# The three score blocks of a head pair: one burst or several on TensorE, in a hybrid decoder layer

## The chip, the cores and the metric

The kernel runs on one core of a Trainium2 chip. The metric is the device time of one execution in microseconds (us); the time of a kernel is the median of its runs. A profiled execution gives a page and a trace, in which every instruction stands with its start, its duration, its line in the kernel's file and what it waited for. The engines are TensorE (matmuls, with its weight loads as a row of their own), VectorE, ScalarE, GpSimd and SyncE, which issues most DMAs. In the profile they are PE, PEld, DVE, ACT, POOL and SP.

## The reference

One layer of a decoder over 1024 positions of 1024 channels, in float32:

```python
h = rms_norm(x, norm_mix)
xa, ga, q, f, v, g, m_a, m_b = split(h @ w_in)
y_a = rg_lru(conv4(xa)) * gelu(ga)                   # recurrence by channel
qf  = silu(q);  f_gate = lb + (1 - lb) * sigmoid(f)  # 8 heads of 128 channels
kf  = (1 - lb) * sigmoid(-f)
o   = hgrn2(qf, kf, log(f_gate), v)                  # gated linear attention
y_b = rms_norm(o) * silu(g)
x   = x + (sigmoid(m_a) * y_a + sigmoid(m_b) * y_b) @ w_out
h   = rms_norm(x, norm_mlp)
x   = x + square(relu(h @ w_up)) @ w_down
return rms_norm(x, norm_final)
```

The part that matters here is `hgrn2`. Per head it is causal attention without a softmax, in which the weight of position s for a later position t is the product of the gates between them:

```python
scores[t, s] = sum_k qf[t, k] * kf[s, k] * prod(f_gate[s+1 .. t, k])   # s <= t
o[t]         = sum_s scores[t, s] * v[s]
```

## The kernel before, in words

**The products.** Matrices are multiplied in float32 out of two parts each, a high one and the rest; `mm3` (line 142) issues the three matmuls of a product, lines 144 to 146. A product over the whole width of 512 columns is 0.4 us long in the trace's rows and starts a little over 0.2 us after the one before.

**The head pairs.** The mixer works on 512 positions (c = 0 or 1) of two heads (p = 0 to 3) at a time. I call these eight pieces of work head pairs and number them 4c + p, 0 to 7. For each there is a `stage(i)` (line 818), a Python generator which projects `v` of the pair before, then `xa`, `q` and `f` of its own pair and the gates of the recurrence, and which yields after every few matmuls; and `hgrn(c, p, ...)` (line 556), which makes the attention of a pair out of the projected `q`, `f` and `v`. The loop at line 942 runs `hgrn` of pair i while stage i + 1 (for pair 7, `last_stage`) is used to fill its gaps: `go(n)` inside `hgrn` lets the stage go on by n yields. A yield is called a step here. In a stage from the second on, the first 16 steps belong to `v` (six matmuls of 256 columns each), the next eight to `xa`, the next eight to `q` (six matmuls of 512 columns each), and so on. TensorE executes exactly in the order in which the Python code issues: `pin` (line 138) ties each of its instructions to the one before.

**The scores.** Inside chunks of 128 positions the scores are put together from blocks at several distances, because the product of gates between two positions is factored into a part on the side of `q` and a part on the side of `k`. Three sets of small matmuls, made by `blocks` (line 563), come first: `pt1` out of `q1` and `kk`, `pt2` out of `qa` and `kb`, `pt8` out of `qb` and `kc`. Each set is 32 matmuls with a stationary block of 32 columns and 48 moving columns; a float32 matmul is two records in the trace, so that a set is a burst of 64 on line 570. VectorE makes the operands: the products on line 560, the last of them for `pt8` in `level_q` (line 623). Afterwards VectorE takes the results out: `own_block(pt1)` (lines 576 to 581), `level_blocks(0, ...)` for `pt2` and `level_blocks(1, ...)` for `pt8` (line 589), between them products that turn `kc` and `qb` into the operands of the next distances (32 and 64, matmuls at lines 690 and 701). These follow after `go(at[1])`; transposes of `k` (line 727), the products `k` by `v` (737) and the output (762, 765) follow at `go(at[2])`, `go(at[3])` and `go(at[4])`.

**PSUM.** Its eight banks go under three tags: `pj` with four (projections), `sc` with two (`pt1`, `pt2`, the blocks of distance 64, one of the four `v` sums, one half of the recurrence's gates), `hg` with two (`pt8`, the blocks of distance 32, all transposes, `k` by `v`, the output). A bank comes free when its last reader is done.

**What else is in a stage.** The second half of the positions is normalised and transposed while the first half is worked on. `transposed` (line 174) takes one tile of 128 rows: four transposes into one bank of `hg`, four into another (line 178); `split` (line 86) then copies each bank's content on ScalarE (line 87) and subtracts the copy from it on VectorE (line 88). In stage 2 this is done for one tile behind the fourth step of `xa`, that is behind step 20, and in stage 3 for two, behind its steps 18 and 22 (`hooks`, line 830). In stage 1 one is done between `xa` and `q`.

**VectorE and ScalarE.** Their order is found by the framework's planner at build time, which takes instructions as they become ready in its own estimate, those traced earlier first, those under `high_priority` (lines 106 and 827) ahead of that.

The steps at which the bursts stand come from tables:

```python
GO = (26, 5, 3, 1, 1)                # pairs 1, 2, 3
GO_FIRST = (16, 5, 2, 1, 2)          # pair 0
GO_SECOND_HALF = (26, 7, 3, 1, 1)    # pairs 4 to 7
```

The first entry is the step of the third burst; the first stands four steps before it, the second two.

## Time and profile before

| | |
|---|---|
| median of 3 runs | 1543.05 us (1542.97 to 1544.44) |
| profiled execution | 1542.76 us |
| its span, first to last instruction | 1541.0 us |
| granted TensorE clock, mean | 0.999 |
| TensorE busy | 1524.6 us, 99% |
| VectorE busy | 1150.3 us, 75% |
| ScalarE busy | 810.2 us, 53% |
| GpSimd busy | 153.8 us, 10% |

A row of the timeline gives start, duration, engine, line, operation, output and inputs, their sizes, and in brackets the idle time before it and what ended that. A row of the groups gives engine, line, operation and shapes with a count, then busy us, the mean ns of one, and the idle time before. Names are those of the program's tiles without their numbers: `sc` is a bank for scores, `xT_x` one for the transposes of `x`. TensorE's rows are pipelined: an instruction starts before the one ahead of it ends, so that the distance of starts is what it costs.

### The profile page before, as it was taken

What the parts mean: (1) busy time and instruction counts of PE and PEld (TensorE: products, weight loads), DVE (VectorE), ACT (ScalarE), POOL (GpSimd) and SP (SyncE); (2) the same over time, 40 slices, a digit from 0 to 9 for tenths busy, and PEclk for the clock granted to TensorE, in tenths of its full rate; (3) what the DMA queues carried; (4) which work ended last, traced back from release to release, by engine and by line L of the source; (5) the groups of instructions that cost most, each with busy time, mean ns of one, the idle gap of its engine ahead of it and who ended that gap; (6) DMA issues with size and microseconds to landing.
All of it is one profiled execution on the core that took longest, in us unless ns stands there. A gap on an engine that the chain in (4) does not pass through costs nothing. (4 is left out here: it accounts for less than half of the span.)

```text
span 1541.0 us, 23190 instructions
## 1 busy us (share of the span) xinstructions
PE 1524.6 (99%) x9081; PEld 1273.8 (83%) x9081; DVE 1150.3 (75%) x1656; ACT 810.2 (53%) x1341; POOL 153.8 (10%) x188
## 2 busy tenths in 40 slices
PE   8999999999999999999999999999999999999997
PEld 7878988889889887888888888888888778888886
DVE  5798595485675838786856578888888898888877
ACT  6656757568567335454533447667767721111115
POOL 1022210232614600000000000000000000000000
PEclk9999999999999999999999999999999999999999
DMA  8545455465664274432338324666666675666642
GB/s 300 188 160 192 151 192 192 150 220 169 228 229 142 99 298 164 150 137 82 137 103 330 127 109 161 264 247 248 249 248 248 231 296 224 244 257 252 250 184 109
DMA packets 81679, 306.82 MB, mean 199 GB/s; under 512 B 8481, under 2 KB 20897, under 8 KB 68642
## 3 DMA queue, kind: packets, MB, share of 16 engines
q1 hardware_dynamic: 77536, 292.75, 51.6%
q10 hardware_dynamic: 4034, 12.59, 2.1%
q8 instruction: 71, 1.16, 0.3%
q14 instruction: 38, 0.31, 0.1%
HBM read 201.50 MB, written 103.81 MB: 198 GB/s over the span
## 5 line engine op out<-in xcount | busy, mean ns | idle before, releaser
L1559 DVE TENSOR_TENSOR acc<-acc,dX 128x512 f32<-128x512 f32 x128 | 85.3, 685 | 29.9 <-PE dX L146 27.4
L87 ACT CAST wA<-q 128x512 fp32r<-128x512 f32 x46 | 28.6, 622 | 147.9 <-PE dX L146 101.6
L88 DVE TENSOR_TENSOR wL<-raw,wH 128x1024 fp32r<-128x1024 f32 x48 | 58.7, 1224 | 43.2 <-ACT wH L87 43.0
L87 ACT CAST wH<-raw 128x1024 fp32r<-128x1024 f32 x48 | 50.4, 1051 | 36.4 <-DMA raw<-wts_in 14.7
L1559 DVE TENSOR_TENSOR acc<-acc,dY 128x512 f32<-128x512 f32 x64 | 43.5, 686 | 13.1 <-PE dY L146 12.9
L144 PE MATMUL po<-wH,y 128*128 128x512 f32 x128 | 49.8, 393 | 0.0
L145 PE MATMUL po<-wL,y 128*128 128x512 f32 x128 | 49.8, 389 | 0.0
L146 PE MATMUL po<-wH,y 128*128 128x512 f32 x128 | 49.7, 390 | 0.0
L1420 ACT ACTIVATE b<-b 128x512 f32<-128x512 f32 x48 | 30.2, 630 | 32.2 <-DVE b L1419 32.1
L88 DVE TENSOR_TENSOR wA<-q,wA 128x512 fp32r<-128x512 f32 x46 | 31.5, 687 | 15.4 <-ACT wA L87 15.3
L108 ACT CAST wH<-raw 128x1024 fp32r<-128x1024 f32 x36 | 37.7, 1049 | 8.2 <-issue 3.7
L171 POOL TENSOR_TENSOR rstd_h<-rstd_h,mhalf 128x1 f32<-128x1 f32 x8 | 4.6, 585 | 371.9 <-DVE rstd_h L166 371.9
L465 DVE SCALAR_TENSOR_TENSOR xc<-xp,pvt,xc 128x512 f32<-128x512 f32 x48 | 40.0, 844 | 1.1 <-ACT xc L449 1.1
L981 DVE TENSOR_TENSOR s<-q,q 128x512 f32<-128x512 f32 x46 | 31.6, 687 | 4.9 <-DMA q<-mlp_in 4.6
L378 POOL TENSOR_TENSOR stt<-r,stt 128x256 fp32r<-128x256 f32 x16 | 19.9, 1262 | 126.3 <-ACT stt L377 114.2
L989 DVE TENSOR_TENSOR s<-q 128x512 f32<-128x512 f32 x46 | 31.6, 687 | 0.4
L1421 ACT ACTIVATE b<-b 128x512 f32<-128x512 f32 x48 | 30.2, 631 | 1.2
L769 ACT ACTIVATE on<-po 128x128 f32<-128x128 f32 x64 | 16.9, 278 | 26.1 <-PE po L765 26.0
L146 PEld LDWEIGHTS po<-wH,y 128*128 128x128 f32 x128 | 24.0, 188 | 5.0
L145 PEld LDWEIGHTS po<-wL,y 128*128 128x128 f32 x128 | 24.1, 188 | 4.8
L144 PEld LDWEIGHTS po<-wH,y 128*128 128x128 f32 x128 | 24.0, 188 | 4.8
L1071 DVE TENSOR_TENSOR gb<-gY,ge 128x512 f32<-128x512 f32 x14 | 9.7, 690 | 23.3 <-PE gY L146 23.3
(2546 smaller groups left out, 5448.6 us busy)
## 6 DMA issues: line engine op xcount, KB each, us to landing
q<-mlp_in SPq DMA_DIRECT2D x92, 512.0 KB, 3.7
raw<-wts_in SPq DMA_DIRECT2D x80, 512.0 KB, 4.7
rest<-wL SPq DMA_DIRECT2D x36, 512.0 KB, 2.8
wL<-rest SPq DMA_DIRECT2D x36, 512.0 KB, 4.0
hd<-ri SPq DMA_DIRECT2D x16, 256.0 KB, 3.5
od<-onT ACTq DMA_DIRECT2D x8, 512.0 KB, 6.9
cdT<-stT SPq DMA_DIRECT2D x16, 256.0 KB, 3.1
o<-od SPq DMA_DIRECT2D x4, 1024.0 KB, 7.3
```

Of the source, the lines that this page charges most:

```text
L87: keep(A.copy(h, src))
L88: ins = V.tensor_tensor(out=lo, in0=src, in1=h.bitcast(F32), op=ALU.subtract)
L108: A.copy(h, raw)
L144: pin(PE.matmul(o, ah, bh, start=first, stop=False, **how))
L145: pin(PE.matmul(o, ah, bl, start=False, stop=False, **how))
L146: pin(PE.matmul(o, al, bh, start=False, stop=last, **how))
L465: ins = V.scalar_tensor_tensor(xc[:, s, :], xp[:, j : j + T], pvt[:, PV_CW + 8 * j + u : PV_CW + 8 * j + u + 1], xc[:, s, :], op0=ALU.mult ...
L981: ins = V.tensor_tensor(out=sa[:, 0, :], in0=a21, in1=a22, op=ALU.add)
L989: V.tensor_tensor(out=sb[:, 0, :], in0=a21, in1=a11, op=ALU.add)
L1420: A.activation(b[:, at, :], b[:, at, :], AF.Relu, scale=-1.0 if at == 2 else 1.0)
L1421: A.activation(b[:, at, :], b[:, at, :], AF.Square)
L1559: V.tensor_tensor(out=dst, in0=dst, in1=banks[bk, pr], op=op)
```

## The change

A table says for six of the eight pairs how many steps to go before the first burst, between the first and the second, and between the second and the third; pairs 3 and 6 take the default. The first number counts from the place where the first burst stood. What is put before the bursts or between them is taken off the steps that follow the third, so that everything behind `go(at[1])` keeps its step.

```diff
+SCORES_AT = {0: (1, 0, 3), 1: (-4, 0, 0), 2: (3, 0, 0), 4: (2, 0, 0), 5: (0, 0, 0), 7: (3, 0, 0)}
...
         at = GO_FIRST if first else GO_SECOND_HALF if c else GO
-        between = 2
-        go(at[0] - 2 * between)
+        before_1, before_2, before_8 = SCORES_AT.get(4 * c + p, (0, 0, 4))
+        go(at[0] - 4 + before_1)
         pt1 = blocks(kk, lambda k: q1[:, 16 * k : 16 * k + 16, :], "1")
-        go(between)
+        go(before_2)
         pt2 = blocks(kb, lambda k: qa[:, k * g0 // 32 : (k + 1) * g0 // 32, 1:7, :], str(c0))
-        go(between)
+        go(before_8)
         pt8 = blocks(kc, lambda k: q4[:, k * g1 // 32 : (k + 1) * g1 // 32, 1:7, :], str(c1), "hg")
...
-        go(at[1])
+        go(at[1] + 4 - before_1 - before_2 - before_8)
```

| pair | bursts at steps, before | after |
|---|---|---|
| 0 | 12, 14, 16 | 13, 13, 16 |
| 1 | 22, 24, 26 | 18, 18, 18 |
| 2 | 22, 24, 26 | 25, 25, 25 |
| 3 and 6 | 22, 24, 26 | 22, 22, 26 |
| 4 | 22, 24, 26 | 24, 24, 24 |
| 5 | 22, 24, 26 | 22, 22, 22 |
| 7 | 22, 24, 26 | 25, 25, 25 |

## The prediction

> **What bounds the kernel now.** I read the page first, its span and its row of engines:

> ```profile
> span 1541.0 us, 23190 instructions
> PE 1524.6 (99%) x9081; PEld 1273.8 (83%) x9081; DVE 1150.3 (75%) x1656; ACT 810.2 (53%) x1341; POOL 153.8 (10%) x188
> ```

> then TensorE's waits from 66 to 560 us, where all eight head pairs lie (the two largest of four; both belong to pair 0),

> ```profile
> PE po L762 <- DVE sn L748: 0.9, 1, 0.9
> PE sc L701 <- DVE qf L560: 0.5, 1, 0.5
> ```

> and the busy times of the stretch behind pair 0 (us, TensorE, its weight loads, VectorE, ScalarE, GpSimd, granted clock):

> ```profile
> 125.00:512.00 387.00, 386.83 (x3555) 335.10 (x3555) 264.24 (x445) 256.14 (x510) 107.98 (x130) 1.00 0.54 184
> ```

> TensorE is busy 99% of the span, and there for 386.83 of 387.00 us at full clock. Its order is written by hand, so time lost between two of its instructions is paid in full, and so is a new wait.

> **What a burst costs.** `L570` is a score block, 64 short matmuls. Around the first one of head pair 1, in the order of time, and the durations of its matmuls:

> ```profile
> 133.13 0.39 PE L144 MATMUL pj_xa<-hT00H,wH 128*128 128x512 f32 x1
> ...
> 135.86 1.03 PE L178 MATMUL xT_x<-ident,xn 128*128 128x128 f32 x8
> ...
> 139.24 0.39 PE L146 MATMUL pj_xa<-hT01H,wL 128*128 128x512 f32 x1
> 139.56 0.89 PE L570 MATMUL sc<-q,kk 128*32 128x48 f32 x64
> 140.38 0.50 PE L144 MATMUL pj_xa<-hT01H,wH 128*128 128x512 f32 x1
> 140.71 0.40 PE L145 MATMUL pj_xa<-hT01L,wH 128*128 128x512 f32 x1
> 140.95 0.39 PE L146 MATMUL pj_xa<-hT01H,wL 128*128 128x512 f32 x1
> ```

> ```profile
> L570 PE MATMUL sc<-q,kk x128: 206/206/230, 447.8 to 509.7; 128*32 128x48 f32 x128
> ```

> Between the 133.13 and 135.86 rows are twelve matmuls of the stream: 2.73 us, 0.227 each. From 139.24 to 140.95 are 1.71 us and three such steps (0.68), so one burst costs 1.03 us. From its first start to its last end are 0.89 us, and one matmul lasts 0.206: 64 starts fill 0.68 us. The other 0.35 us is entry and exit (0.32 to the burst, 0.33 from its successor to the next, in place of 0.227, and what hangs over). A burst that follows another directly should cost 0.68 us and save 0.35. No row shows two in succession, so the bounds are 0 (changing operands costs as much as leaving the stream) and 0.35; I take 0.35, because all three write in the same form of 32 columns.

> **The sum of the gain.** Nothing is removed: 24 bursts stay, and every other instruction, DMAs too. Merges are two each in pairs 1, 2, 4, 5 and 7 and one each in 0, 3 and 6: 13. In pair 0 I count nothing (bounds 0 and 0.35):

> ```profile
> 80.00:104.00 24.00, 23.46 (x326) 18.74 (x325) 24.00 (x50) 8.84 (x14) 4.27 (x5) 1.00 0.51 178
> ```

> VectorE is busy there for 24.00 of 24.00 us, and the waits at `L701` and `L762` above end with its work: a TensorE that comes 0.35 us sooner waits 0.35 us longer. Twelve merges by 0.35 are 4.2 us.

> **Are the operands there?** The third block needs the last product into `qb`. A step of the loop is six matmuls, 1.36 us. VectorE's last products into `qb` in pairs 2, 4, 5 and 7, each with the first burst of its pair:

> ```profile
> 205.91 0.68 DVE L560 TENSOR_TENSOR qb<-qb,seg 128x512 f32<-128x512 f32 x1
> 202.72 0.38 PE L570 MATMUL sc<-q,kk 128*32 128x48 f32 x16
> 324.70 0.67 DVE L560 TENSOR_TENSOR qb<-qb,seg 128x512 f32<-128x512 f32 x1
> 325.50 0.40 PE L570 MATMUL sc<-q,kk 128*32 128x48 f32 x17
> 385.87 0.68 DVE L560 TENSOR_TENSOR qb<-qb,seg 128x512 f32<-128x512 f32 x1
> 386.67 0.42 PE L570 MATMUL sc<-q,kk 128*32 128x48 f32 x20
> 512.21 1.16 DVE L560 TENSOR_TENSOR qb<-qb,seg 128x512 f32<-128x512 f32 x1
> 509.03 0.46 PE L570 MATMUL sc<-q,kk 128*32 128x48 f32 x24
> ```

> The third block starts 1.4 us after the first. Pair 2, moved three steps back: 202.7 + 4.1 + 1.4 = 208.2, ready at 206.6. Pair 4, two: 329.6, ready at 325.4. Pair 5, none: 388.1, ready at 386.6. Pair 7, three: 514.5, ready at 513.4. So no wait, with 1.1 us to spare where it is tightest; a VectorE that slips by more takes back that pair's 0.7 us. In pairs 0, 3 and 6 the third block stays. Behind the bursts, the next score matmuls (`L690`) keep their step, and VectorE's work for them starts no later.

> **Where the change adds a wait.** Only pair 1 is moved ahead, by four steps, and it is moved past something. Stage 2, which fills the gaps of pair 1, has `transposed` (the `L178` row at 135.86) behind its step 20. The three bursts stood at steps 22, 24 and 26; now they stand at 18. The bank tag `hg` has two buffers. The third block takes one and holds it until `level_blocks(1, ...)` has read it, at the end of the score products. The transposes want two, one for each half row. The first half finds the other buffer; the second half must wait until one comes free, with all of TensorE queued behind it.

> When does it come? The triple starts behind the twelve matmuls that end at the 133.13 row and adds 1.03 + 2 x 0.68 = 2.4 us: the transposes start at 138.3, their second half would at 138.7, four by (1.03 - 0.27)/7 = 0.11 us later, where 0.27 is one transpose:

> ```profile
> L178 PE MATMUL xT_x<-ident,xn x8: 270/272/273, 135.9 to 136.6; 128*128 128x128 f32 x8
> ```

> What frees the first half's buffer is a copy on ScalarE, then a subtraction on VectorE:

> ```profile
> 136.78 0.58 ACT L87 CAST hT10H<-xT_x 128x512 fp32r<-128x512 f32 x1
> ```

> ```profile
> 138.18 1.28 DVE L172 SCALAR_TENSOR_TENSOR xn<-x,rstd_x,gain 128x1024 f32<-128x1024 f32 x1 [0.74 <-POOL rstd_x L171]
> 139.38 1.22 DVE L88 TENSOR_TENSOR wL<-raw,wH 128x1024 fp32r<-128x1024 f32 x1
> 140.52 0.68 DVE L88 TENSOR_TENSOR hT10L<-xT_x,hT10H 128x512 fp32r<-128x512 f32 x1
> ```

> From below: the first half ends at 138.9, then 0.58 and 0.68 give 140.1, a wait of 1.4 us. With VectorE's queue as it is, the subtraction ends at 141.2: 2.5 us. With the lag of before (4.7 us, from the end of the first half at 136.5 to 141.2): 143.6, 4.9 us. From above, with all score products of pair 1 in front of it. These are, among VectorE's groups from 133 to 152 us:

> ```profile
> L589 DVE COPY_PREDICATED dd<-mu,sc 128x192 f32<-128x192 uint8 (+2 forms) x4 | 1.4, 350 | 0.0
> L560 DVE TENSOR_TENSOR qb<-qb,seg 128x256 f32<-128x256 f32 (+1 forms) x2 | 1.0, 548 | 0.0
> L560 DVE TENSOR_TENSOR kc<-kc,seg 128x768 f32<-128x768 f32 x1 | 0.9, 950 | 0.0
> L560 DVE TENSOR_TENSOR kk<-kc,seg 128x512 f32<-128x512 f32 x1 | 0.7, 681 | 0.0
> L560 DVE TENSOR_TENSOR qf<-qb,seg 128x512 f32<-128x512 f32 x1 | 0.7, 679 | 0.0
> L581 DVE COPY_PREDICATED dd<-mu,sc 128x128 f32<-128x128 uint8 x1 | 0.4, 442 | 0.0
> L560 DVE TENSOR_TENSOR dd<-sc,mf 128x256 f32<-128x256 f32 x1 | 0.4, 411 | 0.0
> ```

> With `L589` six times that is 2.1 + 1.1 + 0.95 + 0.68 + 0.68 + 0.44 + 0.41 = 6.4 us, so 147.6 and a wait of 8.9 us. I take 3.2: the queue as it is with the first of the products (0.7 us) in front. The subtraction has a high priority in the planner, yet in the rows two operations go first although its copy ended at 137.4.

> The sum is -4.2 + 3.2 = -1.0 us. The profiled execution took 1542.76 us, 1.8 more than its span: 1541.8. The median of the runs is 0.29 above it: 1542.0.

> **Rivals.**
> - No wait, or one near its lower bound. For it: the subtraction's priority, and 0.74 us of idle VectorE before 138.18. Against: two buffers and three users. Without a wait 4.2 to 4.55 us are gained, 1538.7; at 1.4 us, about 1540.0.
> - Slower: the second half gets the third block's buffer, or the subtraction stands behind the products. The wait of 8.9 us makes 4.7 net: 1547.7. The sign turns at a wait of 4.2 us, and at 7.3 it shows. For it: these products are traced ahead of the transposes now. Against: the priority.
> - TensorE runs out of instructions in a triple. The page's instruction queue, what it fetched from 450.2 to 451.5 us, and TensorE behind a burst of pair 6:

> ```profile
> q8 instruction: 71, 1.16, 0.3%
> ```

> ```profile
> q8 instruction: 1, 0.02, 4.6%
> ```

> ```profile
> 448.66 0.50 PE L144 MATMUL pj_xa<-hT11H,wH 128*128 128x512 f32 x1
> 449.00 0.40 PE L145 MATMUL pj_xa<-hT11L,wH 128*128 128x512 f32 x1
> ```

>   71 packets bring 18162 loads and matmuls, 256 in a piece. A triple is 384 of them in 2.05 us; two borders are 256 instructions, 1.37 us, apart, so a triple can want a second piece while it runs. A packet fits into that window of 1.3 us; if each of five triples waited as long, 6.5 us are lost: 1548.5. Against: TensorE left its burst at 448.66 in the usual 0.34 us although the packet came only after 450.2, so a whole piece lay ready. [...]
> - No saving between neighbours: 1546.3 with the wait, 1543.1 without.

> **How the numbers follow.** My forecast (a wait of 1.5 to 7 us, net between -2.7 and +2.8) has 0.54; no wait or a very short one 0.31; the long wait 0.07; starved triples 0.05; no saving 0.03. A measurement here tells 0.2%, 3.1 us, from no change, so faster is under 1540.0 and slower over 1546.1: faster 0.32 (the second case, and a little of the first), same 0.55, slower 0.13. The forecast's own range is 1540.3 to 1545.9; the stated one reaches to the case without a wait, 1538.5, and to 1546.2.

> **What would show it.** In a triple, 192 starts take 2.05 us, with 0.32 us before them and 0.33 after their successor, once. TensorE pauses ahead of the fifth `L178` transpose near 138.7 us, ended by VectorE's `hT10L` or `dd`; the length of the pause decides the sign. `L701` and `L762` of pair 0 wait some 0.35 us more together. I am wrong if the pause is missing, if triples hold gaps near 1 us, or if other pairs wait at their third block.

## The result and the profile after

| | before | after |
|---|---|---|
| median of the runs | 1543.05 us | 1548.87 us (1546.99 to 1550.06, 5 runs) |
| ratio after / before | | 1.0035 (95% interval 1.0025 to 1.0046) |
| profiled execution | 1542.76 us | 1548.87 us |
| its span | 1541.0 us | 1547.1 us |

The change made the kernel 0.35% slower, some 6 us. The forecast was 1542.0 us, no change. Span and engines of the page after:

```profile
span 1547.1 us, 23189 instructions
PE 1523.7 (98%) x9081; PEld 1277.4 (83%) x9081; DVE 1145.9 (74%) x1656; ACT 809.7 (52%) x1341; POOL 147.5 (10%) x188
```

TensorE is busy 0.9 us less than before, in a span 6.1 us longer: it stands idle 7.0 us more. (Matmuls that run slower, as they do below, count as busy and don't show in this difference.) The two largest waits of TensorE from 66 to 560 us, after (total, times, longest):

```profile
PE xT_x L179 <- DVE hT10L L89: 6.0, 1, 6.0
PE pk L728 <- DVE kk L561: 1.1, 1, 1.1
```

Neither was there before. (Lines of the kernel after are one higher than before: the burst is `L571`, the transposes `L179`.)

**The pause in pair 1.** TensorE's timeline after, at the place of the large wait (start, duration):

```profile
138.76 0.60 PE L179 MATMUL xT_x<-ident,xn 128*128 128x128 f32 x4
145.40 1.11 PE L179 MATMUL xT_x<-ident,xn 128*128 128x128 f32 x4 [6.04 <-DVE hT10L L89]
146.17 0.78 PE L145 MATMUL pj_xa<-hT01H,wH 128*128 128x512 f32 x1
146.74 0.63 PE L146 MATMUL pj_xa<-hT01L,wH 128*128 128x512 f32 x1
...
151.01 0.45 PE L147 MATMUL pj_xa<-hT01H,wL 128*128 128x512 f32 x1
```

The first four transposes start at 138.76, the fifth at 145.40, where the prediction had it stop. But it stops twice as long as forecast (6.2 us in place of 3.2), and something unforeseen follows: between the rows at 146.74 and 151.01 ten steps take 4.27 us, 0.427 each in place of 0.227. The busy times by stretch show why (columns as in the prediction; the number behind the five engines is the granted clock):

```profile
139.00:145.40 6.40, 0.36 (x5) 0.12 (x3) 6.13 (x12) 2.67 (x4) 0.00 (x0) 0.91 0.67 251
145.40:151.30 5.90, 5.90 (x17) 4.79 (x18) 2.96 (x7) 1.63 (x3) 2.92 (x7) 0.52 0.53 181
151.30:163.00 11.70, 11.70 (x53) 9.68 (x52) 7.68 (x10) 5.37 (x7) 2.28 (x4) 1.00 0.42 148
```

For 5.9 us behind the pause TensorE runs at a clock of 0.52, then at 1.00 again. So pair 1 pays twice. At the next score matmuls it is 8.2 us later than before. Its two merges are taken as 0.7 us saved, at the price of the other pairs; with 6.2 us of pause, 2.7 us are left for the half clock (ten steps at 0.2 more are 2.0 of them, the rest are the transposes and the matmuls at both ends).

What TensorE waits for is the subtraction `hT10L` on VectorE, which needs the copy `hT10H` on ScalarE. ScalarE's timeline after:

```profile
140.65 0.62 ACT L669 COPY kk<-kc 128x512 f32<-128x512 f32 x1 [6.06 <-DVE kc L561]
141.92 0.62 ACT L670 COPY qf<-qb 128x512 f32<-128x512 f32 x1 [0.65 <-DVE qb L561]
142.45 1.04 ACT L88 CAST wH<-raw 128x1024 fp32r<-128x1024 f32 x1
143.39 0.58 ACT L88 CAST hT10H<-xT_x 128x512 fp32r<-128x512 f32 x1
```

and VectorE's:

```profile
139.67 0.94 DVE L561 TENSOR_TENSOR kc<-kc,seg 128x768 f32<-128x768 f32 x1
140.53 1.02 DVE L561 TENSOR_TENSOR qb<-qb,seg 128x256 f32<-128x256 f32 x2
...
143.52 1.22 DVE L89 TENSOR_TENSOR wL<-raw,wH 128x1024 fp32r<-128x1024 f32 x1 [0.23 <-ACT wH L88]
144.66 0.68 DVE L89 TENSOR_TENSOR hT10L<-xT_x,hT10H 128x512 fp32r<-128x512 f32 x1
145.26 0.95 DVE L590 COPY_PREDICATED dd<-mu,sc 128x192 f32<-128x192 uint8 x3
```

The first half of the transposes ended before 139.4. Its copy starts 4 us later, although ScalarE had stood idle for 6.06 us: the head of ScalarE's queue was a copy of the scores (`kk`), and that waited for VectorE's product into `kc`. So 6.06 us of idle ScalarE were of no use to the copy behind that head. The delay reaches the subtraction over VectorE too: `hT10H` ends at 143.97, but `wL` stands in front of `hT10L` until 144.7, and it waited for `wH` on ScalarE, which stood behind the same two copies.

**The wait in pair 7.** The first row of each fence is the first taking out of a score block, the last is the product into `kk` for which `L728` waits. VectorE before:

```profile
515.70 0.41 DVE L560 TENSOR_TENSOR dd<-sc,mf 128x256 f32<-128x256 f32 x1
...
531.69 0.68 DVE L560 TENSOR_TENSOR kk<-kk,seg 128x512 f32<-128x512 f32 x1
```

and after:

```profile
526.29 0.42 DVE L561 TENSOR_TENSOR dd<-sc,mf 128x256 f32<-128x256 f32 x1
...
539.49 0.68 DVE L561 TENSOR_TENSOR kk<-kk,seg 128x512 f32<-128x512 f32 x1
```

The kernel is some 6 us late there. The taking out starts 10.6 us later than before, that is 4.5 us later in the loop, three steps of TensorE's (4.1 us) and a little. The product comes 7.8 us later, so 2 us of the delay are left when TensorE wants it.

**The account.** Differences of start times between the two traces, at the same instructions of TensorE:

| part | predicted | measured |
|---|---|---|
| up to the first projections of pair 0 (24 us) | - | +0.9 |
| pair 0 | 0 | -0.4 (burst -0.32, given back +0.30; a wait of 0.33 for the transposes of the output is gone) |
| merges of pairs 1 to 7 | -4.2 | -3.6 |
| pause in pair 1 | +3.2 | +6.2 |
| half clock behind it (what is left of pair 1) | - | +2.7 |
| wait in pair 7 | 0 | +1.4 |
| behind 560 us | - | -1.1 |
| sum | -1.0 | +6.1 |

The first row is no part of the change: in the profiles of the experiments it is between -0.3 and 2.5 us, with the same work up to there. The last is mostly a wait that the before had at 1241 us and that a later kernel does not meet. Between 1235 and 1245 us, before:

```profile
PE dY L146 <- DVE u15t L88: 1.4, 1, 1.4
```

After, no wait for `u15t` is left there, and the difference falls by 1.73 us.

### The profile page after: what moved, and what is told of

It reads as the page before. It is cut to its first block, busy times and chain, and to the rows that moved or that the text cites. A ratio compares the mean times of both kernels' runs of the same rounds, so it can differ in the third digit from the quotient of the medians.

```text
span 1547.1 us, 23189 instructions
## 1 busy us (share of the span) xinstructions
PE 1523.7 (98%) x9081; PEld 1277.4 (83%) x9081; DVE 1145.9 (74%) x1656; ACT 809.7 (52%) x1341; POOL 147.5 (10%) x188
## 3 DMA queue, kind: packets, MB, share of 16 engines
q8 instruction: 71, 1.16, 0.3%
## 5 line engine op out<-in xcount | busy, mean ns | idle before, releaser
L88 ACT CAST wA<-q 128x512 fp32r<-128x512 f32 x46 | 28.6, 622 | 147.6 <-PE dX L147 101.6
L88 ACT CAST wH<-raw 128x1024 fp32r<-128x1024 f32 x48 | 50.4, 1050 | 40.0 <-DMA raw<-wts_in 15.3
L145 PE MATMUL po<-wH,y 128*128 128x512 f32 x128 | 49.9, 394 | 0.0
L146 PE MATMUL po<-wL,y 128*128 128x512 f32 x128 | 49.9, 390 | 0.0
L172 POOL TENSOR_TENSOR rstd_h<-rstd_h,mhalf 128x1 f32<-128x1 f32 x8 | 4.6, 583 | 371.8 <-DVE rstd_h L167 371.8
L145 PEld LDWEIGHTS po<-wH,y 128*128 128x128 f32 x128 | 24.1, 188 | 4.8
L146 PEld LDWEIGHTS po<-wL,y 128*128 128x128 f32 x128 | 24.1, 188 | 4.7
```

What stands on the lines that cost most here:

```text
L88: keep(A.copy(h, src))
L145: pin(PE.matmul(o, ah, bh, start=first, stop=False, **how))
L146: pin(PE.matmul(o, ah, bl, start=False, stop=False, **how))
```

## The experiments

Each ratio is to runs of the kernel before on the same chip at the same time, with a 95% interval. `SCORES_AT` of the kernel after is `{0: (1, 0, 3), 1: (-4, 0, 0), 2: (3, 0, 0), 4: (2, 0, 0), 5: (0, 0, 0), 7: (3, 0, 0)}`.

### Without the move of pair 1

```diff
-SCORES_AT = {0: (1, 0, 3), 1: (-4, 0, 0), 2: (3, 0, 0), ...
+SCORES_AT = {0: (1, 0, 3), 2: (3, 0, 0), ...
```

> The changed kernel, with pair 1 alone at the default (first two bursts together at step 22, the third at step 26, behind the transposes). Theory (the pause in pair 1 is the third block's hold on a bank of hg, and the slow matmuls behind the pause are its consequence): TensorE's pause of 6.2 us ahead of the fifth transpose and the eleven matmuls at 0.427 us behind it are both gone; pair 1 goes from 8.24 us longer than before to 0.35 us shorter, so 1548.9 - 8.6 = 1540.3 us. Rival (the bursts' new places upset VectorE's order in general, and the pause only shows it): a pause of several us turns up elsewhere and the time stays above 1545 us.

Measured: 1541.63 us against 1542.57, ratio 0.9993 (0.9984 to 1.0003). TensorE's largest wait from 66 to 560 us:

```profile
PE pk L728 <- DVE kk L561: 1.4, 2, 1.1
```

No pause and no half clock, as expected. The time is 1.3 us over the 1540.3 expected. 0.7 us of it are small new delays of pair 1 with its first two blocks together (a wait of 0.3 for `kk` among them): the pair is 0.4 us longer than before, not 0.35 shorter. The rest is not accounted for; the wait of pair 7 is still there, but the number expected held it. Undoing the move of pair 1 takes back 7.2 us (1548.87 to 1541.63), or 6.8 with each taken against its own runs of before.

### The move of pair 1 alone

```diff
-SCORES_AT = {0: (1, 0, 3), 1: (-4, 0, 0), 2: (3, 0, 0), ...
+SCORES_AT = {i: (-4, 0, 0) if i == 1 else (0, 2, 2) for i in range(8)}
```

> The kernel before, with pair 1 alone changed: its three bursts at step 18; all other pairs with three bursts as before. Theory (pair 1 carries the whole loss): 1543.05 + 8.2 = 1551.3 us, with the same pause near 139 us and the same slow matmuls behind it. Rival (the loss comes from the sum of the other pairs too, for instance the new 1.3 us wait in pair 7): under 1549 us.

Measured: 1549.55 us against 1542.57, ratio 1.0042 (1.0027 to 1.0057).

```profile
PE xT_x L179 <- DVE hT10L L89: 7.2, 1, 7.2
```

Pair 1 loses 8.7 us by itself, and little else changes up to 1240 us (0.4 us come back); there 1.73 us come back as in the kernel after, which the expectation had left out.

### The third block behind the transposes

```diff
-SCORES_AT = {0: (1, 0, 3), 1: (-4, 0, 0), ...
+SCORES_AT = {0: (1, 0, 3), 1: (-4, 0, 8), ...
```

> The changed kernel, with pair 1's first two bursts at step 18 as in the change, but its third at step 26, behind the transposes. Theory (it is the bank of the third block, not the early place of the bursts): no pause at the transposes, 1548.9 - 8.6 = 1540.3 us, like the kernel with pair 1 at the default. Rival (score work that comes to VectorE and ScalarE ahead of the copy and the subtraction delays them, whichever bursts stand there): the transposes still pause for 2 us or more, 1543 us or more.

Measured: 1544.19 us against 1542.57, ratio 1.0010 (1.0001 to 1.0019). The pause is gone, as it must be if the third block's bank is what the transposes lack. But the time is not: the third block now comes late, and pair 1 waits three times behind it. TensorE, around the last of these waits:

```profile
164.77 0.39 PE L147 MATMUL pj_f<-hT00H,wL 128*128 128x512 f32 x1
167.00 2.56 PE L738 MATMUL pkv<-v,kT 128*128 128x128 f32 x16 [1.85 <-ACT kT L733]
169.79 0.63 PE L146 MATMUL pj_f<-hT00L,wH 128*128 128x512 f32 x1
170.22 0.63 PE L147 MATMUL pj_f<-hT00H,wL 128*128 128x512 f32 x1
```

2.2 us from start to start were followed by the half clock (steps of 0.43 us). So the time expected, 1540.3, is missed: a later third block trades one pause for another.

### The transposes two steps later

```diff
-        hooks = {at: ... for at, n in {2: ((4, 1),), 3: ((2, 2), (6, 3))}.get(i, ())}
+        hooks = {at: ... for at, n in {2: ((6, 1),), 3: ((2, 2), (6, 3))}.get(i, ())}
```

> The changed kernel with the transposes of stage 2 two steps (2.7 us) later, pair 1 still at step 18. Theory: the end of the pause is set by ScalarE and VectorE, whose queues hold copies and products of the scores in front of the copy hT10H and the subtraction hT10L, not by the place of the transposes. Then the subtraction still ends near 145.3 us and the wait shrinks from 6.2 to about 3.5 us. If a pause of more than 2 us is followed by matmuls at half clock, as behind the waits of 6.2 us (changed kernel) and 2.2 us (third block eight steps later), these stay and cost some 1.7 us: 1545.7 us. Without them 1544.0. Rival: the copy moves along with the transposes, the wait stays near 6 us: 1548.9.

Measured: 1545.65 us against 1542.53, ratio 1.0024 (1.0013 to 1.0034). The number is met, the reason isn't:

```profile
PE xT_x L179 <- DVE dd L590: 4.9, 1, 4.9
```

The wait shrank by 1.1 us in this execution, not by 2.7, and it ends with `dd`, the taking out of the third block. The planner gave VectorE another order, in which the score work starts 1.7 us later (the product into `kc` at 141.34 in place of 139.67), and the second half took the third block's bank, which came free before the first half's. This execution took 1549.16 us, the longest of its seven (the shortest 1544.03); 2.0 us of it are a wait far behind, at 1031 us. So the end of the pause is not fixed in time; it moves with VectorE's queue.

### Part of the score work behind the transposes

```diff
+        go(3)                       # pair 1 alone; taken off go(at[1])
-        mul(k4(kc, c1)[:, :, 0:3, :], ...)
+        behind(mul(k4(kc, c1)[:, :, 0:3, :], ...), hT10L)
-        A.copy(pairs(kk)[:, :, 1, :], pairs(kc)[:, :, 1, :])
+        behind(A.copy(pairs(kk)[:, :, 1, :], pairs(kc)[:, :, 1, :]), hT10H)
```

`behind` stands for an order without a semaphore between two instructions of one engine. The `go(3)` only puts the transposes ahead of the score products in the program; TensorE's own order stays.

> The changed kernel, in which for pair 1 alone the program issues the transposes ahead of the score products, VectorE's product into kc is tied behind the subtraction hT11L's pair of the first half, and ScalarE's copy into kk behind the copy of the first half. Theory: the score work in front of the copy and of the subtraction makes the pause as long as it is. Without it the wait is 1.4 to 2.5 us, as the bounds of the prediction from the queue without the score products have it, no slow matmuls follow, and the time is 1541.6 (pair 1 at its default) + 0.8 = 1542.4 us; a little more if the score products, now later, are waited for in pair 1 at L691 or L728. Rival: something else holds the bank; the wait stays near 6 us and the time near 1548.9.

Measured: 1546.70 us against 1542.53, ratio 1.0025 (1.0014 to 1.0035). The expectation missed. ScalarE, with lines shifted by the edit:

```profile
142.14 0.62 ACT L686 COPY qf<-qb 128x512 f32<-128x512 f32 x1 [6.18 <-DVE qb L571]
142.66 1.04 ACT L94 CAST wH<-raw 128x1024 fp32r<-128x1024 f32 x1
143.61 0.58 ACT L94 CAST hT10H<-xT_x 128x512 fp32r<-128x512 f32 x1
```

With the copy into `kk` out of the way, the other copy, into `qf`, stood at the head of the queue and waited just as long. TensorE's pause was 4.9 us between starts and ended again with `dd`, in an execution of 1548.89 us, the longest of its eight.

### All of the score work behind the transposes

```diff
+        behind(mul(k4(kc, c1)...), hT10L)       # and both products into qb
+        behind(first taking out of pt1, hT10L)
+        behind(A.copy(kk ...), hT10H)           # and the copy into qf
```

> The changed kernel in which all of pair 1's work behind its triple is tied behind the first half of the transposes: VectorE's taking out of the first block and the products into kc and qb behind the subtraction hT10L, ScalarE's two copies of the scores behind the copy hT10H. In the run that moved only kc and one copy, the other copy (into qf) still stood in front of hT10H on ScalarE and the pause was 4.9 us. Theory: with both queues clear the pause is the prediction's 'queue as it is', xn and wL in front of hT10L: it ends near 141 us, a wait of 2 to 2.7 us in place of 6.0. At this length it is at the edge of the half clock (2.2 us was followed by it, 1.5 us not). Pair 1's later waits at L691, L702 or L728 grow, since its scores come 3 us later: 1542.5 to 1546. Rival: the pause is not made by the order of these two queues: it stays at 4.5 us or more.

Measured: 1544.29 us against 1542.26, ratio 1.0013 (1.0004 to 1.0022). TensorE's wait and VectorE's rows:

```profile
PE xT_x L187 <- DVE hT10L L96: 2.3, 1, 2.3
```

```profile
138.29 1.28 DVE L181 SCALAR_TENSOR_TENSOR xn<-x,rstd_x,gain 128x1024 f32<-128x1024 f32 x1 [0.74 <-POOL rstd_x L180]
140.59 1.23 DVE L96 TENSOR_TENSOR wL<-raw,wH 128x1024 fp32r<-128x1024 f32 x1 [1.02 <-ACT wH L94]
141.74 0.68 DVE L96 TENSOR_TENSOR hT10L<-xT_x,hT10H 128x512 fp32r<-128x512 f32 x1
```

2.3 us, inside the 2 to 2.7 expected, and the time is inside its range too. This is the prediction's "queue as it is" of 2.5 us: `xn` and `wL` in front, nothing of the scores. So the other 3.7 us of the 6.0 are the order of the two queues. Even this pause brought the half clock, for seven matmuls (0.50 from 143.7 to 147 us). No experiment got rid of the pause altogether: with the triple at step 18 the bank is short by one.

### All three blocks together wherever the operands allow

```diff
+SCORES_AT = {0: (1, 0, 3), 1: (0, 0, 0), 2: (3, 0, 0), 3: (0, 0, 0),
+             4: (0, 0, 0), 5: (0, 0, 0), 6: (0, 0, 0), 7: (3, 0, 0)}
```

> Three bursts together wherever the operands are there, whatever the borders of the instruction pieces: pairs 1, 3, 4, 5 and 6 at step 22, 2 and 7 at step 25; pair 0 as in the change. 15 merges in all, 14 without pair 0. Theory without instruction fetch (a merge gives 0.33 us wherever it stands): 1543.05 + 1.4 (the new wait in pair 7) - 14 x 0.33 = 1539.8 us, and triples without gaps. Rival (a triple in which two borders of the instruction pieces fall waits for a fetch, about 1 us each in pairs 1, 3, 4 and 6): gaps of about 1 us inside those four triples, about 1543.5 us.

Measured: 1551.77 us against 1542.57, ratio 1.0065 (1.0048 to 1.0083). TensorE's waits from 66 to 560 us begin with

```profile
PE sc L571 <- issue: 4.2, 2, 2.9
PE pj_xa L146 <- issue: 3.1, 1, 3.1
PE pj_xa L145 <- issue: 1.9, 1, 1.9
```

"issue": nothing that the trace shows is waited for. Pairs 1, 3, 4 and 6 stop inside or right behind their triple, pairs 2, 5 and 7 don't. This is what the third rival would look like, instructions that do not come in time (the packets that bring them are read below); but the kernel after itself has no wait on "issue" from 66 to 560 us. TensorE in pair 6 of this run:

```profile
456.17 0.54 PE L571 MATMUL sc<-qb,kc 128*32 128x48 f32 x32
459.61 0.68 PE L571 MATMUL sc<-qb,kc 128*32 128x48 f32 x32 [2.90 <-issue]
460.22 0.80 PE L145 MATMUL pj_xa<-hT11H,wH 128*128 128x512 f32 x1
```

Behind this stall, too, the clock is halved (0.50 from 460 to 463 us), as behind that of pair 3. Neither expected time came near: the stalls are where the rival had them, but 1.5 to 3.6 us between two starts in place of about 1.

### Places mixed

```diff
+SCORES_AT = {0: (1, 0, 3), 1: (0, 2, 2), 2: (3, 0, 0), 4: (2, 0, 0), 5: (0, 0, 0)}
```

> The changed kernel with pair 1 at its old places (steps 22, 24, 26) and pair 7 at the default (22, 22, 26); the triples of pairs 2, 4 and 5 stay, as do the pairs of bursts in 0, 3 and 6. Theory: the wait of 1.1 to 1.4 us of pair 7 for kk at L728 comes from moving its first burst three steps back, by which VectorE starts the work behind it 4 us later. Then it is gone here, and pair 1 loses nothing: 1542.6 less 0.66 + 0.27 + 0.69 (pairs 2, 4, 5) less 3 x 0.35 = 1539.9 us. Rival: the wait comes with any merge in pair 7 (TensorE is early, VectorE's queue is full): 1541.2.

Measured: 1539.01 us against 1542.53, ratio 0.9979 (0.9970 to 0.9988): faster than before. The wait for `kk` in pair 7 is gone:

```profile
530.18 0.68 DVE L561 TENSOR_TENSOR kk<-kk,seg 128x512 f32<-128x512 f32 x1
```

1.5 us earlier than before the change (531.69), and TensorE, itself 1.8 us earlier there, does not wait. So the wait came with moving that burst back and not with any merge in pair 7. All three blocks together at the old place of pair 7 were not run. The table's entry for pair 1 is its old places. Pair 4 alone does not gain (+0.14): its triple has small gaps, 3.02 us from the first start to its successor's in place of 2.19.

### Borders moved, places kept

```diff
-            for n in range(8):
+            for n in [*range(8)] * (2 if name == "1" and nm == "10" else 1):   # pt1 of pair 4
```

on the kernel with mixed places (the condition, a small function in the kernel, is written out here).

> The kernel with mixed places, in which pair 4 makes the 64 matmuls of its first burst twice, the second time over the first. This costs 0.7 us by itself and moves every later border of TensorE's instruction pieces 128 instructions ahead, while no burst changes its place. The triple of pair 5 then has its borders at about its 104th and 360th instruction in place of 232 and before the start. Theory that TensorE runs out of instructions where the borders fall badly: one pause of 1.5 to 4 us with nothing waited for in the triple of pair 5 or right behind it, and 1542 to 1544.5 us. Theory that the stalls seen with triples everywhere came from the places in the loop: no pause in pair 5, 1540.6 us.

Measured: 1554.59 us against 1542.53, ratio 1.0077 (1.0063 to 1.0091). Pair 5, whose bursts stand where they stood:

```profile
395.35 0.44 PE L574 MATMUL sc<-qb,kc 128*32 128x48 f32 x21
398.94 1.17 PE L574 MATMUL sc<-qb,kc 128*32 128x48 f32 x43 [3.16 <-issue]
```

Of the queue that brings instructions, one packet comes in this pause, between 396.6 and 397.7 us:

```profile
q8 instruction: 1, 0.02, 5.3%
```

3.2 us are lost in a triple that runs without a gap in the kernel with mixed places. Pair 4 itself, four bursts long now, stops for 4.9 us, which the expectation had not thought of; with the half clock behind both stalls (0.52 from 336 to 341 us, behind that of pair 4) this makes the time longer than expected. In pair 5 only the count of the instructions ahead differs (and it comes 7.8 us later, behind the stall of pair 4), so the place in the loop is not the cause; what is left is where the borders of the instruction pieces fall.

The borders can be counted, with pieces of 256 taken from the trace of before (18162 loads and matmuls in 71 packets, 255.8 each). I number TensorE's instructions (loads, matmuls and the few that only wait or signal) through the program. All stalls lie at numbers that leave 193 to 197 when divided by 256 (193 or 194 in a count of the trace's records alone). With 192 taken as the border, its place within the burst, and the longest distance of two starts there:

| kernel, pair | borders at instruction | longest distance, us |
|---|---|---|
| triples anywhere, 1 | 124, 380 | 2.07 |
| triples anywhere, 3 | 129, 385 | 3.58 |
| triples anywhere, 4 | 19, 275 | 1.55 |
| triples anywhere, 6 | 63, 319 | 3.11 |
| borders moved, 4 (four bursts) | -5, 251, 507 | 5.13 |
| borders moved, 5 | 41, 297 | 3.36 |
| after, 1, 2, 5, 7 | one: 190, 204, 171, 179 | none |
| after, 4 | -3, 253 | 0.15 (small gaps, 0.4 in all) |

A triple is some 385 instructions. Two borders inside it are 1.37 us apart (256 at the 5.3 ns of a burst), and in all six cases the stall is at the second; with one inside (four triples of the kernel after) there is none. That is the sense of the places in the change.

The traces also show what came ahead of the end of each stall. In all six, and in the seventh below, one packet of the instruction queue ends 1.3 to 1.5 us before TensorE goes on (in the case above at 397.6, TensorE at 398.9). The stall is as long as that packet is late: it starts between 0.9 us before TensorE stops and 2.8 us after.

### One border

```diff
-SCORES_AT = {0: (1, 0, 3), 1: (0, 2, 2), 2: (3, 0, 0), 4: (2, 0, 0), 5: (0, 0, 0)}
+SCORES_AT = {0: (1, 0, 3), 1: (0, 2, 2), 2: (3, 0, 0), 3: (-1, 0, 0), 4: (3, 0, 0), 5: (0, 0, 0)}
```

> The kernel with mixed places, pair 4 one step later (25, 25, 25) and pair 3 with all three blocks at step 21. Counted from the program's start, all six long stalls so far (1.5 to 5.1 us) lie at positions 193 to 197 of 256 of TensorE's instructions, always at the second such border inside one burst. Pair 4 had the borders at -5 and 251 of its triple, with 0.5 us of small gaps, and comes to -17 and 239; pair 3, which stalled for 3.4 us with borders at 129 and 385, comes to -115, 141 and 397, one inside. Theory of the borders: neither stalls, pair 4 gains 0.6 us and pair 3 0.35: 1539.0 - 0.9 = 1538.1 us. Rival: pair 3 does not bear a triple at all, by its operands (qb comes 0.1 us ahead) or by its place: a wait of 1 us or more in it, 1539.5 us or more.

Measured: 1540.83 us against 1542.26, ratio 0.9992 (0.9983 to 1.0001). The time expected, 1538.1, is missed. Pair 4 does what was expected, -0.70 us without a gap. Pair 3 has no wait on operands but stalls after all:

```profile
PE pj_xa L146 <- issue: 1.6, 1, 1.6
```

seven matmuls behind its triple, at the border 397, which I had counted as outside. TensorE gets there only some 1.5 us after the triple's end and still stops. So "two borders in one triple" is too narrow a rule: it seems to be the time between two borders that counts. By the starts it was 3.2 us here (141 to 397) and too short; the 6.0 us in pair 5 of the kernel after (171 to 427) were enough. Even that is not the whole rule: in pair 4 of the kernel after the borders -3 and 253 are 1.4 us apart, and no start there is more than 0.15 us late. There a packet came from 333.5 to 334.5 us, ahead of the triple, which starts at 335.95.

### Pair 4 one step later

```diff
-SCORES_AT = {0: (1, 0, 3), 1: (0, 2, 2), 2: (3, 0, 0), 4: (2, 0, 0), 5: (0, 0, 0)}
+SCORES_AT = {0: (1, 0, 3), 1: (0, 2, 2), 2: (3, 0, 0), 4: (3, 0, 0), 5: (0, 0, 0)}
```

> The kernel with mixed places, pair 4 alone one step later (25, 25, 25), pair 3 as before that (22, 22, 26). In the run with both moved, pair 4 took 0.70 us less than before the change in place of 0.14 more, and pair 3 lost 1.8 us behind its triple. Theory of the borders: pair 4's gain stays and pair 3's loss goes, 1539.0 - 0.8 = 1538.2 us, with no wait on nothing at L571 or behind it. Rival: pair 4's gain came from what pair 3's stall did to the work before it; then its small gaps of 0.5 us come back, 1539.0.

Measured: 1539.37 us against 1543.74, ratio 0.9971 (0.9962 to 0.9981). No wait on "issue" is left among TensorE's from 66 to 560 us, and pair 4's triple is in the trace as it should be:

```profile
329.10 0.89 PE L571 MATMUL sc<-q,kk 128*32 128x48 f32 x64
329.80 0.86 PE L571 MATMUL sc<-qa,kb 128*32 128x48 f32 x64
330.52 0.89 PE L571 MATMUL sc<-qb,kc 128*32 128x48 f32 x64
331.34 0.50 PE L145 MATMUL pj_q<-hT10H,wH 128*128 128x512 f32 x1
```

The differences to the trace of before are now -0.69, -0.35, -0.65, -0.70, -0.33 and -0.34 us for pairs 2 to 7: nine merges, 3.06 us, 0.34 each. Against its own runs of before it gains 4.4 us and the kernel with mixed places 3.5; the intervals of the two overlap, so they can't be told apart. Both beat before and after.

## Why the prediction was wrong, and where it was right

The sum came out 7.1 us too low (-1.0 against +6.1): 3.0 us by the pause in pair 1, 2.7 by the half clock behind it, 1.4 by the wait in pair 7 and 0.6 by the merges; the other rows of the table add up to -0.6. The longer pause alone would have stayed in the range, at 1545.0 us. The two terms that were put at nothing took the time out of it.

**The price of a merge: right.** 0.35 us each was the term, and 0.34 is measured over nine merges. In the kernel after twelve gave 3.6 us in place of 4.2 (with pair 1's two taken as 0.7); what lacks is mostly pair 4's 0.4 us, lost in small gaps around its second border (-3 and 253).

**Pair 0: right.** Its merge brought -0.32 and the waits behind it took +0.30. They came at the score matmuls on `L691` (`L690` before), which wait 0.3 us for `qb`, not at the two later lines that the prediction named.

**The pause in pair 1: right place, wrong size. This is the first step that failed.** "I take 3.2: the queue as it is with the first of the products (0.7 us) in front." Measured were 6.2 us, inside the 1.5 to 7 us that the forecast allowed, but 3.0 over the term. The step looked at VectorE's queue alone and trusted the priority of the subtraction. The copy `hT10H` on ScalarE it counted with its 0.58 us, and never asked what stands in front of it there: the copy stood behind two copies of the scores that waited for VectorE's products. With all score work behind the transposes on both engines, the wait is 2.3 us; the 2.5 of the "queue as it is" was a good number for a queue that this program does not have. The rival with the products in front (8.9 us) had VectorE's order nearly right; three of its takings out ran behind the subtraction, so it was not reached.

**What a pause costs beyond itself: put at nothing, the second step that failed.** In the kernel after it is 2.7 us at the half clock. Of the eleven pauses of 2.2 us and more in these profiles, ten went with such a stretch. The trace of before has no pause from 66 to 560 us that could have shown it (its longest wait there is 0.9 us). The prediction, whose range for the wait was 1.5 to 7 us, had no term for it. The length alone doesn't tell which pause is followed by one: the clock fell behind pauses of 2.23 and 2.60 us between starts, and not behind one of 2.40.

**"The next score matmuls keep their step, VectorE's work for them starts no later": wrong for pair 7, the third step that failed.** Moved three steps back, the first block comes out of its bank 4.5 us later in the loop, and TensorE waits 1.1 us (1.4 between starts) for `kk`. I checked only that the operands were ready ahead of the burst, not that the work behind it had the slack. At its old place there is no wait. Pair 2, moved by the same three steps, had it.

**Operands ready, no wait at a third block: right**, in all pairs.

**Starved triples: wrong for this kernel, seen in others.** The rival put 1.3 us on each of five triples. In the kernel after four of the five have one border inside and run without a gap, and pair 4, with one just ahead of it and one inside, loses 0.4 us; where two fell into one burst, the pauses were 1.5 to 5.1 us, more than the rival's price. The 1.3 us were an estimate from one packet of the trace of before, and how far ahead of TensorE the pieces come, no run shows. In that trace, where no burst follows another directly, all borders are crossed without a stall: none of TensorE's waits there is on "issue". At 5.3 ns an instruction without a break (1.37 us for 256) that did not always hold.

**The end.** 1.7 of the loss came back at 1241 us, where before had a wait of 1.4 us of its own. The prediction summed its terms as if all of them reached the end; without this piece of luck its number would have been off by 1.7 us more.

## What to carry to other kernels

Before moving work of TensorE past an instruction that needs a bank, follow the chain that frees the bank over every engine in it, and put on each queue what the moved work itself will release there; an idle engine may be of no use until the head of its queue can run (ScalarE here, idle for 6.06 us). Price a pause of 2.2 us and more with slow matmuls behind it, as ten of the eleven here had them (2.7 us in the kernel after), and a move back with the slack of the work behind it. Merging short bursts was worth the entry and exit of each (0.34 us), as long as no stall on instructions came with it (1.5 to 5.1 us).

## What the runs showed of the hardware

- **Half clock behind a pause.** Behind the first 24 us of these profiles TensorE has eleven pauses of 2.2 us and more between two starts. Ten of them, of 2.23 to 7.50 us, went with a stretch at a granted clock of 0.5, in which a matmul of 512 columns takes 0.427 us in place of 0.227. In six of the ten TensorE waited for a semaphore, in four (in pairs 3 and 6 with triples anywhere, 4 and 5 with the borders moved) on "issue". The eleventh, 2.40 us in the run with the transposes two steps later, had none: the clock stays at 1.00, and behind its first matmul, the row below, the next ones follow at 0.22 to 0.34 us. Pauses up to 2.07 us had none either. So no single length divides the two.

```profile
1033.80 0.50 PE L145 MATMUL uX<-h2T3H,ws35H 128*128 128x512 f32 x1 [2.01 <-ACT e L1417]
```
